# A decoder layer on one core: seven products added up in one PSUM bank, three big PSUM tiles, and changes of order and mode

## The chip, the core and the metric

One core of a Trainium2 chip runs the whole program. The metric is the device time of one execution in microseconds (us), the median of several runs. TensorE (PE) does the matrix products, VectorE (DVE) and ScalarE (ACT) read its results in PSUM, GpSimd (POOL) and SyncE (SP) issue most of the transfers from HBM. PSUM has eight banks of 512 float32 columns on 128 partitions.

## What is computed

One decoder layer on 256 tokens of width 2048 in float32, with all weights read once (about 450 MB):

```python
h = rmsnorm(x, norm_mix)
proj = h @ w_in                        # 30 column blocks of 512, the last 12 are the gates
ya, yb, yr = diff_attention(...), conformer_conv(...), retention(...)
merged = sum(sigmoid(gate_i) * (y_i @ w_branch[i]))
x = x + merged @ w_out
x = x + cross_attention(rmsnorm(x), rmsnorm(mem))   # w_q, w_kv, w_o; 4 heads of 512
a, b = split(rmsnorm(x) @ w13); x = x + (silu(a) * b) @ w2     # hidden 5632
return rmsnorm(x, norm_final)
```

## The kernel before, in words

A weight matrix is cut into blocks of 512 columns (`nb`), each into chunks of 512 rows (`c`), each chunk into halves of 2 x 128 rows. A float32 product is made as three: a value is split into a high part in the engine's reduced format and the rest, and TensorE adds high x high, high x low and low x high in PSUM. So every half of a chunk that arrives as a tile `raw` (512 KB) is cast by ScalarE to `wh` (`hi_of`) and its rest is made by VectorE as `wl` (`lo_of`); five buffers of each (`hlp`) and ten of `raw` (`rawp`) stand between the transfers and TensorE. The activations are the other operand, split in the same way (`Act.hi`, `.lo`).

The program is a list of *units*: a unit is the weights of one half-chunk and its products. `run_items` goes through them; before a unit's products the weights of up to four more units are prepared (`LA = 4`), and after each unit `pump` advances every background *task* (a Python generator: transposes, attention, convolution, normalisation) by one step. A task that holds small PSUM tiles (`TP`, pool `pst`) says so with the number that it yields; `cap` limits their sum, and `drain` runs a task to its end when its result is needed. From this emission order, and the priorities that it gives, a planner lays down the order on each engine before the run; only instructions marked `keep_in_program_order` (the transfers of `ld` on SP and of `gd` on POOL) hold the written order on their engine.

A plain unit ("N") multiplies a half-chunk with both halves of the tokens: 12 products of 512 columns. `block` runs one column block of plain units into a big PSUM tile `mm` (two banks, pool `psm`); `pair_n` runs two column blocks side by side. `pair` runs two column blocks with some chunks ("S", two of four in `MODES2 = "SSNN"`) as a *quad*: seven units of 6 products on sums and differences of the four half-chunks in place of the 48 plain products. The weights' sums come from two additions on VectorE (`f2`, `f3`) and two accumulating transfers on POOL's queue (`gd(..., accum_op=ALU.add)` in `f2` and `f6`); those of the activations are made once by `factors`. Products 2, 3 and 4 of a quad go to the big tiles `ps0` and `ps1`; products 1, 5, 6, 7 go to small tiles of their own (`pp`), and `join1` to `join7` add them together on VectorE into SBUF tiles, to which `done` adds the big tile. There are 26 such pairs: 5 for the gates, 4 for the cross-attention's keys and values, 2 for `w_out`, 1 for `w_o`, 10 in `w_13` and 4 in `w_2`.

PSUM is divided into two big tiles (4 banks) and four small ones (4 banks). `rstd_of` makes an inverse root with one VectorE instruction and a power on GpSimd.

Of the kernel before, what the change touches and what calls it, by code (L numbers as in the profile page):

```python
# [16 lines left out]
D = 2048  # L17
# [40 lines left out]
def trunk(ctx, tc, xT, xtok, memT, memtok, w_in, w_br, w_out, w_q, w_kv, w_o, w_13, w_2,  # L58
# [64 lines left out]
    cap = [4]  # L123
# [169 lines left out]
    def products(u, only=None, final=True):  # L293
        a = u["act"]
        for k in range(2):
            for ps, key, k0, t, kind in u["prods"]:
                if only is not None and t not in only:
                    continue
                ah, al = lhs(a, kind, (t, k0) if kind == "n" else t, k)
                o = ps[key]  # L300
                fl = (id(ps), key)
                pe.matmul(o, ah, u["hi"][:, k, :], start=fl in u["start"] and k == 0, stop=False)
                pe.matmul(o, ah, u["lo"][:, k, :], start=False, stop=False)
                pe.matmul(o, al, u["hi"][:, k, :], start=False, stop=fl in u["stop"] and k == 1)
# [27 lines left out]
    def quad_jobs(pp, ps0, ps1, w0, w1, a):  # L332
# [3 lines left out]
        def unit(ps, key, k0, t, kind, fn, **w):  # L336
            def add():
                load(**w)
                u = add_unit([(ps, key, k0, t, kind)], a)
                u["alloc"] = alloc_tp1 if ps is pp else alloc_mm  # L340
# [3 lines left out]

        def alloc_tp1(ps, key):
            ps[key] = TP()
# [58 lines left out]
    def pair(W0, W1, acts, modes, evac0, evac1):  # L405


        ps0, ps1, pp = {}, {}, {}
# [5 lines left out]
        def enter():  # L414
            settle(3)
            cap[0] = 3
            pin[0] = True

        def join1():
            x0, x1 = S4([P, 2, 512]), S4([P, 2, 512])  # L420
            xs.extend([x0, x1])
            sc.copy(x0[:, 0, :], pp.pop(1))

        def join5():
            ve.tensor_tensor(out=xs[1][:, 1, :], in0=pp.pop(5), in1=xs[0][:, 0, :], op=ALU.add)

        def join6():

            p = pp.pop(6)
            ve.tensor_tensor(out=xs[1][:, 0, :], in0=p, in1=xs[1][:, 1, :], op=ALU.subtract)  # L430
            ve.tensor_tensor(out=xs[0][:, 1, :], in0=p, in1=xs[0][:, 0, :], op=ALU.subtract)

        def join7():
            p = pp.pop(7)
            ve.tensor_tensor(out=xs[0][:, 1, :], in0=p, in1=xs[0][:, 1, :], op=ALU.subtract)
            ve.tensor_tensor(out=xs[1][:, 1, :], in0=xs[1][:, 0, :], in1=p, op=ALU.subtract)
            cap[0] = 4

        def done(n, ps, evac):
            def f():  # L440
                x = xs[n]
                ve.tensor_tensor(out=x, in0=ps["m"], in1=x, op=ALU.add)
                xs[n] = None
                insb[0] = True
                evac(x)
                insb[0] = False
            return f

        call(enter)
        quads = [quad_jobs(pp, ps0, ps1, W0[c], W1[c], acts[c]) for c in sset]  # L450
        n0, n1 = (each_half(ps, [W[c] for c in nset], [acts[c] for c in nset]) for ps, W in ((ps0, W0), (ps1, W1)))

        def units_of(*names):
            return [q[n] for m in names for q in quads for n in m]

        first = units_of(("p1",), ("p2", "p5"), ("p3", "p6"))
        marks = {len(quads) - 1: join1, 3 * len(quads) - 1: join5, 5 * len(quads) - 1: join6}

        def marked(i, f):
            def g():  # L460
                u = f()
                if i in marks:
                    call(marks[i])
                return u
            return g

        us += mixed([marked(i, f) for i, f in enumerate(first)], n0)
        us += [f() for f in units_of(("p7",))]
        call(join7)
        us += mixed(units_of(("p4",)), n1[:len(n1) // 2])  # L470
        call(done(0, ps0, evac0))
        us += [f() for f in n1[len(n1) // 2:]]
        call(done(1, ps1, evac1))

        def unpin():
            pin[0] = False

        call(unpin)
# [36 lines left out]
    def rstd_of(dst, src, scale, w):  # L515
# [3 lines left out]
        nc.gpsimd.tensor_tensor(out=dst, in0=v, in1=nhalf[:, :w], op=ALU.pow)  # L519
# [74 lines left out]
    def factors(a, q):  # L594
# [4 lines left out]
        for o, x, y, op in ((0, a22, a21, ALU.subtract), (2, a11, a21, ALU.subtract),  # L599
                            (1, a22, fv[:, 2], ALU.add), (3, a12, fv[:, 1], ALU.subtract)):  # L600
# [95 lines left out]
    def tok_stats(src, dst, eng):  # L696
# [10 lines left out]
        rstd_of(dst, ss, 1.0 / D, 2)  # L707
# [130 lines left out]
    def conv_norm():  # L838
# [10 lines left out]
        rstd_of(rs, mv.rearrange("p (t s) -> p t s", t=2)[:, :, 1], 1.0, 2)  # L849
# [23 lines left out]
    def win(n0, n1, modes, evac0, evac1):  # L873
# [3 lines left out]
        else:  # L877
# [699 lines left out]
```

## Time and profile before

| what | value |
|---|---|
| time, median of 3 runs | 2031.65 us (2030.2 to 2033.77) |
| the profiled execution | 2031.24 us, its span 2029.5 us |
| TensorE busy | 1990.1 us, 9069 products and transposes |
| VectorE busy | 1680.8 us |
| ScalarE busy | 1122.2 us |
| GpSimd busy | 133.1 us |
| granted TensorE clock, mean | 0.991 |
| read from HBM | 451.73 MB |

Busy time is the union of an engine's instructions. Products overlap in the pipeline (each shows some 0.39 us and the next starts before its end), so a busy TensorE is not one at its peak; an idle figure in square brackets stands before the instruction that ended the wait, with what released it. All compute instructions carry the line of a helper (L86, L94), so groups are told apart by the tiles' names: `wh`, `wl` and `raw` are weights, `mm` and `tp` the big and the small PSUM tiles, `s` SBUF work tiles, `cst_t` the identity for transposes.

### The profile page before, as it was taken

What the parts mean: (1) busy time and instruction counts of PE and PEld (TensorE: products, weight loads), DVE (VectorE), ACT (ScalarE), POOL (GpSimd) and SP (SyncE); (2) the same over time, 40 slices, a digit from 0 to 9 for tenths busy, and PEclk for the clock granted to TensorE, in tenths of its full rate; (3) what the DMA queues carried; (4) which work ended last, traced back from release to release, by engine and by line L of the source; (5) the groups of instructions that cost most, each with busy time, mean ns of one, the idle gap of its engine ahead of it and who ended that gap; (6) DMA issues with size and microseconds to landing.
All of it is one profiled execution on the core that took longest, in us unless ns stands there. A gap on an engine that the chain in (4) does not pass through costs nothing.

```text
span 2029.5 us, 25287 instructions
## 1 busy us (share of the span) xinstructions
PE 1990.1 (98%) x9069; PEld 1641.5 (81%) x9069; DVE 1680.8 (83%) x2049; ACT 1122.2 (55%) x1344; POOL 133.1 (7%) x176
## 2 busy tenths in 40 slices
PE   9999999999999999999999999998999999999998
PEld 7788888888788887778888888886888888878886
DVE  6996689777887787988988565898988899889974
ACT  6434343547465556555656554665655566555653
POOL 0000000000100001011010000100011101011000
PEclk9999999999999999999999999998999999999999
DMA  9555555554677788689999643967899888998891
GB/s 370 189 194 188 176 181 165 181 168 149 176 220 239 243 257 248 226 240 280 284 279 307 208 159 125 288 184 212 226 283 297 257 260 237 289 295 258 262 318 67
DMA packets 128861, 465.97 MB, mean 230 GB/s; under 512 B 14432, under 2 KB 14688, under 8 KB 128736
## 3 DMA queue, kind: packets, MB, share of 16 engines
q1 hardware_dynamic: 105552, 380.46, 53.2%
q0 software_dynamic: 23040, 83.90, 19.5%
q8 instruction: 71, 1.16, 0.2%
q14 instruction: 54, 0.44, 0.1%
q10 hardware_dynamic: 144, 0.01, 0.0%
HBM read 451.73 MB, written 12.58 MB: 229 GB/s over the span
## 4 chain that ended last, share of the span: by engine, by line
PE 50%; issue 9%; DVE 6%; DMA 5%; POOL 1%; ACT 1%; ACTq 0%; POOLq 0%; DVEq 0%
PE mm L86 38%; PE tp L86 12%; DMA raw<-in_w 4%; DVE wl L86 3%; DVE s L86 3%; DMA raw<-in_w_out 1%; DVE raw L86 1%; ACT wh L86 1%; POOL raw L94 1%; DMA s<-in_memtok 0%; DMA raw<-in_w_in 0%; ACT s L86 0%; ACTq L1572 0%; POOL s L94 0%; POOL x2d L94 0%
## 5 line engine op out<-in xcount | busy, mean ns | idle before, releaser
L86 PE MATMUL mm<-wh,s 128*128 128x512 f32 x4528 | 1440.1, 393 | 22.5 <-ACT wh L86 8.7
L86 ACT CAST wh<-raw 128x1024 fp32r<-128x1024 f32 (+1 forms) x861 | 893.6, 1051 | 754.3 <-PE mm L86 462.7
L86 DVE TENSOR_TENSOR wl<-raw,wh 128x1024 fp32r<-128x1024 f32 (+1 forms) x861 | 1030.1, 1220 | 265.2 <-ACT wh L86 252.0
L86 PEld LDWEIGHTS mm<-wh,s 128*128 128x128 f32 x4528 | 854.5, 189 | 204.8 <-ACT wh L86 13.5
L86 PE MATMUL mm<-wl,s 128*128 128x512 f32 x2264 | 889.5, 393 | 7.6 <-DVE wl L86 7.4
L86 PEld LDWEIGHTS mm<-wl,s 128*128 128x128 f32 x2264 | 428.0, 189 | 100.7 <-DVE wl L86 13.2
L86 PE MATMUL tp<-wh,s 128*128 128x512 f32 x896 | 298.5, 392 | 0.0
L86 PEld LDWEIGHTS tp<-wh,s 128*128 128x128 f32 x896 | 168.2, 188 | 34.7 <-issue 0.3
L86 PE MATMUL tp<-wl,s 128*128 128x512 f32 x448 | 174.5, 389 | 0.0
L86 DVE TENSOR_TENSOR s<-s,s 128x1024 f32<-128x1024 f32 (+4 forms) x144 | 141.4, 990 | 5.8 <-ACT s L86 4.0
L86 DVE TENSOR_TENSOR raw<-raw,raw 128x1024 f32<-128x1024 f32 x104 | 126.0, 1220 | 0.5
L86 DVE TENSOR_TENSOR s<-tp,s 128x512 f32<-128x512 f32 (+1 forms) x166 | 110.0, 685 | 19.0 <-PE tp L86 14.2
L86 DVE SCALAR_TENSOR_TENSOR s<-s,prm_t,s 128x256 fp32r<-128x256 f32 (+24 forms) x256 | 105.5, 469 | 0.0
L86 DVE TENSOR_TENSOR s<-mm,s 128x1024 f32<-128x1024 f32 (+1 forms) x71 | 84.4, 1190 | 21.7 <-PE mm L86 21.3
L86 PEld LDWEIGHTS tp<-wl,s 128*128 128x128 f32 x448 | 84.2, 188 | 16.8
L86 ACT ACTIVATE s<-s 128x512 f32<-128x512 f32 (+1 forms) x60 | 46.2, 771 | 64.3 <-DVE s L86 53.9
L94 POOL DMA_DIRECT2D raw<-in_w x56 | 49.4, 882 | 439.4 <-DVE wl L86 187.9
L86 PE MATMUL tp<-cst_t,s 128*128 128x128 f32 x408 | 57.2, 273 | 0.0
L86 PEld LDWEIGHTS tp<-cst_t,s 128*128 128x128 f32 x408 | 48.7, 141 | 9.2 <-issue 0.5
L86 PE MATMUL tp<-s,s 128*128 128x256 f32 (+4 forms) x348 | 54.1, 314 | 0.0
L86 PEld LDWEIGHTS tp<-s,s 128*128 128x128 f32 (+1 forms) x348 | 46.4, 189 | 5.9 <-issue 0.7
L86 ACT COPY s<-tp 128x512 f32<-128x512 f32 (+1 forms) x69 | 35.8, 529 | 21.5 <-PE tp L86 20.0
(88 smaller groups left out, 499.3 us busy)
## 6 DMA issues: line engine op xcount, KB each, us to landing
raw<-in_w SPq DMA_DIRECT2D x264, 512.0 KB, 6.7
raw<-in_w_in SPq DMA_DIRECT2D x239, 512.0 KB, 4.5
raw<-in_w_kv SPq DMA_DIRECT2D x64, 512.0 KB, 6.3
raw<-in_w POOLq DMA_DIRECT2D x56, 512.0 KB, 8.5
raw<-in_w_br SPq DMA_DIRECT2D x48, 512.0 KB, 5.9
raw<-in_w_out SPq DMA_DIRECT2D x32, 512.0 KB, 7.8
raw<-in_w_q SPq DMA_DIRECT2D x32, 512.0 KB, 4.9
raw<-in_w_o SPq DMA_DIRECT2D x32, 512.0 KB, 4.0
```

The lines of the kernel that those rows point to most:

```text
L86: i = f(*a, **k)
L94: tc.keep_in_program_order(nc.gpsimd.dma_start(**kw))
```

## The change

- PSUM becomes three big tiles (6 banks) and two small ones (2 banks); `cap` is 2 throughout.
- In `pair`, products 1, 6, 7 and 4 of the quads go one after the other to the same bank, bank 1 of `ps1`, and product 5 to bank 1 of `ps0`. Between them the bank is copied by ScalarE (`keep1`, `keep5`, `keep6`, `keep7`); `done0` and `done1` combine the copies with the final sums. The two column blocks and the signs in `factors` are exchanged to fit. The units of a pair get a new order: products 1, 2, 5, 3 and the first 6 of both quads come without plain units between them.
- The second pair of start blocks (columns 9 and 7) runs as `pair_n` on the input that is not yet normalised, with the scale applied when the result is read; the normalised input `xn` is made during it.
- One chunk of the first key-value pair and one of the second `w_13` pair become plain (`MODES1 = "SNNN"`).
- `rstd_of` becomes a generator: two rounds pass between VectorE's step and the power, and the power keeps its place in the program order.
- In the last stage three column blocks sum up in big tiles and one in two small tiles, which are claimed once the last hidden chunk is ready.

```diff
-    psm = ctx.enter_context(tc.tile_pool(name="psm", bufs=2, space=bass.MemoryType.PSUM))
+    psm = ctx.enter_context(tc.tile_pool(name="psm", bufs=3, space=bass.MemoryType.PSUM))
-    pst = ctx.enter_context(tc.tile_pool(name="pst", bufs=4, space=bass.MemoryType.PSUM))
+    pst = ctx.enter_context(tc.tile_pool(name="pst", bufs=2, space=bass.MemoryType.PSUM))
-    cap = [4]
+    cap = [2]
...
-                pe.matmul(o, al, u["hi"][:, k, :], start=False, stop=fl in u["stop"] and k == 1)
+                pe.matmul(o, al, u["hi"][:, k, :], start=False, stop=(fl in u["stop"] or "ends" in u) and k == 1, **sk)
...
-        return dict(p1=unit(pp, 1, 0, 0, "n", f1, b11=w0[:, 0:2, :]),
-                    p2=unit(ps0, 0, 2, 0, "n", f2, b21=b21, b12=w1[:, 0:2, :]), p5=unit(pp, 5, 0, 0, "s", f5),
-                    p3=unit(ps1, 0, 0, 3, "s", f3, b22=b22), p6=unit(pp, 6, 0, 1, "s", f6),
-                    p7=unit(pp, 7, 0, 2, "s", f7), p4=unit(ps0, 1, 2, 1, "n", f4))
+        return dict(p1=unit(c1, 1, 0, 0, "n", f1, b11=w0[:, 0:2, :]),
+                    p2=unit(c1, 0, 2, 0, "n", f2, b21=b21, b12=w1[:, 0:2, :]), p5=unit(c2, 1, 0, 0, "s", f5),
+                    p3=unit(c2, 0, 0, 3, "s", f3, b22=b22), p6=unit(c1, 1, 0, 1, "s", f6),
+                    p7=unit(c1, 1, 0, 2, "s", f7), p4=unit(c1, 1, 2, 1, "n", f4))
...
+        def keep1():
+            xs.extend([S4([P, 2, 512]), S4([P, 2, 512])])
+            sc.copy(xs[1][:, 0, :], ps1[1])
+        def keep5():
+            sc.copy(xs[0][:, 0, :], ps0[1])
+        def keep6():
+            sc.copy(xs[1][:, 1, :], ps1[1])
+            ve.tensor_tensor(out=xs[0][:, 0, :], in0=xs[0][:, 0, :], in1=xs[1][:, 1, :], op=ALU.subtract)
+        def keep7():
+            sc.copy(xs[0][:, 1, :], ps1[1])
+        def done0():
+            x = xs[0]
+            ve.tensor_tensor(out=x[:, 0, :], in0=ps0[0], in1=x[:, 0, :], op=ALU.add)
+            ve.tensor_tensor(out=x[:, 1, :], in0=ps0[1], in1=x[:, 1, :], op=ALU.subtract)
...
+        def done1():
+            x = xs[1]
+            ve.tensor_tensor(out=x[:, 0, :], in0=ps1[0], in1=x[:, 0, :], op=ALU.add)
+            sc.copy(x[:, 1, :], ps1[1])
...
+        quads = [quad_jobs(ps1, ps0, W1[c], W0[c], acts[c]) for c in sset]
...
+        us += [f() for f in ending("p1")]
+        call(keep1)
+        us += [f() for f in units_of("p2") + ending("p5")]
+        call(keep5)
+        us += [f() for f in units_of("p3")]
+        p6 = ending("p6")
+        us += mixed(p6[:-1], n0[:-3]) if len(p6) > 1 else [f() for f in n0[:-3]]
+        us.append(p6[-1]())
+        call(keep6)
+        us.append(n0[-3]())
+        us += [f() for f in ending("p7")]
+        call(keep7)
+        us += [f() for f in n0[-2:]]
+        call(done0)
+        us += mixed(units_of("p4"), n1[:len(n1) // 2])
         us += [f() for f in n1[len(n1) // 2:]]
+        call(done1)
...
         ve.tensor_scalar(out=v, in0=src, scalar1=scale, scalar2=EPS, op0=ALU.mult, op1=ALU.add)
-        nc.gpsimd.tensor_tensor(out=dst, in0=v, in1=nhalf[:, :w], op=ALU.pow)
+        yield
+        yield
+        tc.keep_in_program_order(nc.gpsimd.tensor_tensor(out=dst, in0=v, in1=nhalf[:, :w], op=ALU.pow))
...
-        for o, x, y, op in ((0, a22, a21, ALU.subtract), (2, a11, a21, ALU.subtract),
-                            (1, a22, fv[:, 2], ALU.add), (3, a12, fv[:, 1], ALU.subtract)):
+        for o, x, y, op in ((0, a21, a22, ALU.subtract), (2, a11, a21, ALU.subtract),
+                            (1, fv[:, 0], a11, ALU.subtract), (3, a12, fv[:, 1], ALU.add)):
...
-    pair_n([w_in[8, c] for c in range(4)], [w_in[6, c] for c in range(4)], xa, ev_cb(0, rsx), ev_ca(0, rsx),
-           normalise(xa, xn, Rstd(rsx, lambda: drain(st_task)), (), 1))
-    win(9, 7, MODES0, ev_cb(1), ev_ca(1))
+    for n, after in ((0, lambda c: None),
+                     (1, normalise(xa, xn, Rstd(rsx, lambda: drain(st_task)), ()))):
+        pair_n([w_in[8 + n, c] for c in range(4)], [w_in[6 + n, c] for c in range(4)], xa,
+               ev_cb(n, rsx), ev_ca(n, rsx), after)
...
-            pair(w0, w1, mm, MODES2, ev_kv(dst[h]), ev_kv(dst[h + 1]))
+            pair(w0, w1, mm, MODES2 if m or h else MODES1, ev_kv(dst[h]), ev_kv(dst[h + 1]))
...
-                pair(w0, w1, x2n, MODES2, ev_a(i), ev_b(i))
+                pair(w0, w1, x2n, MODES1 if i == 1 else MODES2, ev_a(i), ev_b(i))
...
     def alloc_tp(ps, key):
+        need(hT[10])
+        settle(0)
         ps[0], ps[1] = TP(), TP()
...
-                             alloc=alloc_mm if nb < 2 else alloc_tp))
+                             alloc=alloc_mm if nb < 3 else alloc_tp))
```

For a pair with two quads (a, b) and four plain units for each column block (n, m) the order of the units is, before: 1a 1b 2a n 5a 2b n 5b 3a 6a n 3b 6b n 7a 7b 4a m 4b m m m; after: 1a 1b 2a 2b 5a 5b 3a 3b 6a n 6b n 7a 7b n n 4a m 4b m m m.

## Rows read from the trace of the kernel before

**Rows 1.** The page, busy time of each engine: us, share, count.
```profile
PE 1990.1 (98%) x9069; PEld 1641.5 (81%) x9069; DVE 1680.8 (83%) x2049; ACT 1122.2 (55%) x1344; POOL 133.1 (7%) x176
```

**Rows 2.** Chain in order of time, two steady pairs: start us, us, what.
```profile
1453.99 2.72 PE tp L86 x12
...
1495.72 2.72 PE tp L86 x12
```

**Rows 3.** Windows: stretch, length, each engine's busy us, granted clock, DMA share, GB/s.
```profile
50.00:64.00 14.00, 9.34 (x30) 7.16 (x29) 12.15 (x12) 7.57 (x8) 0.00 (x0) 0.76 0.63 229
543.00:562.00 19.00, 14.27 (x53) 10.81 (x52) 11.98 (x20) 7.45 (x9) 2.51 (x2) 0.82 0.55 148
842.00:874.00 32.00, 26.32 (x103) 19.91 (x102) 28.81 (x34) 14.94 (x18) 2.59 (x3) 0.84 0.65 165
1386.00:1420.00 34.00, 25.22 (x98) 19.97 (x97) 27.16 (x29) 15.18 (x15) 1.70 (x2) 0.85 0.71 219
1453.99:1495.72 41.73, 41.73 (x190) 34.61 (x189) 37.71 (x36) 25.51 (x26) 4.60 (x6) 1.00 0.85 254
```

**Rows 4.** Timeline of TensorE: start us, us, instruction, count, [idle before <-releaser].
```profile
51.78 0.62 PE L86 MATMUL mm<-wh,s 128*128 128x512 f32 x2
...
52.46 0.39 PE L86 MATMUL mm<-wh,s 128*128 128x512 f32 x1
57.51 0.79 PE L86 MATMUL mm<-wh,s 128*128 128x512 f32 x1 [4.66 <-ACT s L86]
...
58.53 1.05 PE L86 MATMUL mm<-wh,s 128*128 128x512 f32 x2
```

**Rows 5.** Timeline of ScalarE at the same place.
```profile
56.19 1.26 ACT L86 ACTIVATE s<-mm,rsx 128x512 f32<-128x512 f32 x2
```

**Rows 6.** Timeline of GpSimd, 528 to 547 us.
```profile
528.88 0.86 POOL L94 DMA_DIRECT2D raw<-in_w_in  x1 [14.54 <-DVE wl L86]
545.35 1.66 POOL L519 TENSOR_TENSOR tn<-tn,nhalf 128x8 f32<-128x8 f32 x1 [15.61 <-DVE tn L86]
546.97 0.89 POOL L94 DMA_DIRECT2D raw<-in_w_in  x1
```

**Rows 7.** Timelines of ScalarE and TensorE, 554 and 555 us.
```profile
554.15 4.83 ACT L86 CAST wh<-raw 128x1024 fp32r<-128x1024 f32 x5 [12.89 <-DMA raw<-in_w_in]
...
555.25 0.80 PE L86 MATMUL mm<-wh,s 128*128 128x512 f32 x1 [3.59 <-ACT wh L86]
```

**Rows 8.** Timeline of TensorE, first key-value pair.
```profile
866.01 0.80 PE L86 MATMUL mm<-wh,s 128*128 128x512 f32 x1 [2.08 <-ACT s L86]
```

**Rows 9.** Groups by shape in one steady pair, VectorE and ScalarE: count, busy us, mean ns.
```profile
L86 DVE TENSOR_TENSOR wl<-raw,wh 128x1024 fp32r<-128x1024 f32 x22 | 26.1, 1220 | 2.9 <-ACT wh L86 2.8
L86 DVE TENSOR_TENSOR raw<-raw,raw 128x1024 f32<-128x1024 f32 x4 | 4.8, 1219 | 0.0
L86 DVE TENSOR_TENSOR s<-tp,s 128x512 f32<-128x512 f32 x4 | 2.7, 686 | 0.8 <-PE tp L86 0.8
L86 DVE TENSOR_TENSOR s<-mm,s 128x1024 f32<-128x1024 f32 x2 | 2.4, 1220 | 0.2 <-PE mm L86 0.2
...
L86 ACT CAST wh<-raw 128x1024 fp32r<-128x1024 f32 x22 | 23.1, 1053 | 15.2 <-PE mm L86 9.7 <-DMA raw<-in_w 2.1 <-PE tp L86 1.4
...
L86 ACT COPY s<-tp 128x512 f32<-128x512 f32 x1 | 0.6, 597 | 0.0
```

**Rows 10.** Timelines of GpSimd, ScalarE, VectorE and TensorE, 1379 to 1412 us.
```profile
1379.25 0.85 POOL L94 DMA_DIRECT2D raw<-in_w  x1 [6.01 <-DMA raw<-in_w]
...
1388.73 3.91 ACT L86 CAST wh<-raw 128x1024 fp32r<-128x1024 f32 x4 [6.14 <-DMA raw<-in_w]
...
1410.51 2.35 DVE L86 TENSOR_TENSOR s<-mm,s 128x1024 f32<-128x1024 f32 x2
...
1411.87 0.76 PE L86 MATMUL mm<-wh,s 128*128 128x512 f32 x1 [7.02 <-DVE s L86]
```

**Rows 11.** The page, issues of accumulating transfers: count, KB each, us to landing.
```profile
raw<-in_w POOLq DMA_DIRECT2D x56, 512.0 KB, 8.5
```

More of the change, by code (lines that the diff above doesn't have):

```diff
@@ L301, in products @@
                 fl = (id(ps), key)
-                pe.matmul(o, ah, u["hi"][:, k, :], start=fl in u["start"] and k == 0, stop=False)
-                pe.matmul(o, ah, u["lo"][:, k, :], start=False, stop=False)
-                pe.matmul(o, al, u["hi"][:, k, :], start=False, stop=fl in u["stop"] and k == 1)
+                sk = dict(skip_group_check=True) if ps.get("open") and key == 1 else {}
+                pe.matmul(o, ah, u["hi"][:, k, :], start=fl in u["start"] and k == 0, stop=False, **sk)
+                pe.matmul(o, ah, u["lo"][:, k, :], start=False, stop=False, **sk)
+                pe.matmul(o, al, u["hi"][:, k, :], start=False, stop=(fl in u["stop"] or "ends" in u) and k == 1, **sk)
     def emit_unit(i):
@@ L343, in unit @@
             return add
-        def alloc_tp1(ps, key):
-            ps[key] = TP()
         b21, b22 = w0[:, 2:4, :], w1[:, 2:4, :]
@@ L396, in f4 @@
             parts(u, t.pop("a"))
[L398 to L401 removed]
+        return dict(p1=unit(c1, 1, 0, 0, "n", f1, b11=w0[:, 0:2, :]),
+                    p2=unit(c1, 0, 2, 0, "n", f2, b21=b21, b12=w1[:, 0:2, :]), p5=unit(c2, 1, 0, 0, "s", f5),
+                    p3=unit(c2, 0, 0, 3, "s", f3, b22=b22), p6=unit(c1, 1, 0, 1, "s", f6),
+                    p7=unit(c1, 1, 0, 2, "s", f7), p4=unit(c1, 1, 2, 1, "n", f4))
     insb = [False]
     def pair(W0, W1, acts, modes, evac0, evac1):
[L408 removed]
+        ps0, ps1 = {"open": True}, {"open": True}
         xs = []
@@ L412, in pair @@
         nset = [c for c in range(len(acts)) if modes[c] == "N"]
[L414 to L447, printed above, removed]
@@ L449, in pair @@
-        call(enter)
-        quads = [quad_jobs(pp, ps0, ps1, W0[c], W1[c], acts[c]) for c in sset]
+        def keep1():
[8 more added lines that the diff above has]
+            sc.copy(xs[0][:, 1, :], ps1[1])
@@ new lines, in done0 @@
+        def done0():
+            x = xs[0]
+            ve.tensor_tensor(out=x[:, 0, :], in0=ps0[0], in1=x[:, 0, :], op=ALU.add)
+            ve.tensor_tensor(out=x[:, 1, :], in0=ps0[1], in1=x[:, 1, :], op=ALU.subtract)
+            xs[0] = None
+            insb[0] = True
+            evac0(x)
+            insb[0] = False
+        def done1():
+            x = xs[1]
+            ve.tensor_tensor(out=x[:, 0, :], in0=ps1[0], in1=x[:, 0, :], op=ALU.add)
+            sc.copy(x[:, 1, :], ps1[1])
+            xs[1] = None
+            insb[0] = True
+            evac1(x)
+            insb[0] = False
@@ L451, in pair @@
+        call(lambda: pin.__setitem__(0, True))
+        quads = [quad_jobs(ps1, ps0, W1[c], W0[c], acts[c]) for c in sset]
         n0, n1 = (each_half(ps, [W[c] for c in nset], [acts[c] for c in nset]) for ps, W in ((ps0, W0), (ps1, W1)))
         def units_of(*names):
[L454 to L463, printed above, removed]
-                return u
-            return g
@@ L467, in pair, with ending, last @@
[L467 to L471, printed above, removed]
+            return [q[n] for n in names for q in quads]
+        def ending(name):
+            fs = units_of(name)
+            def last():
+                u = fs[-1]()
+                u["ends"] = True
+                return u
+            return [f for f in fs[:-1]] + [last]
@@ L472, in pair @@
+        us += mixed(units_of("p4"), n1[:len(n1) // 2])
         us += [f() for f in n1[len(n1) // 2:]]
[L473 to L478, printed above, removed]
+        call(done1)
+        call(lambda: pin.__setitem__(0, False))
         close(us)
@@ L706, in tok_stats @@
         ve.tensor_reduce(out=ss, in_=parts.rearrange("p n t -> p t n"), op=ALU.add, axis=AX.X)
-        rstd_of(dst, ss, 1.0 / D, 2)
+        yield from rstd_of(dst, ss, 1.0 / D, 2)
     def start_task():
@@ L848, in conv_norm @@
         rs = TN(2)
-        rstd_of(rs, mv.rearrange("p (t s) -> p t s", t=2)[:, :, 1], 1.0, 2)
+        yield from rstd_of(rs, mv.rearrange("p (t s) -> p t s", t=2)[:, :, 1], 1.0, 2)
         yield
@@ L969, in ret_task @@
         rs = TN(8)
-        rstd_of(rs, mv.rearrange("p (t s) -> p t s", s=2)[:, :, 1], 1.0, 8)
+        yield from rstd_of(rs, mv.rearrange("p (t s) -> p t s", s=2)[:, :, 1], 1.0, 8)
         yield
@@ L1065, in diff_task @@
         rs = TN(8)
-        rstd_of(rs, ms, 1.0 / P, 8)
+        yield from rstd_of(rs, ms, 1.0 / P, 8)
         yield
@@ L1208, in gen2 @@
                         ve.tensor_reduce(out=ss, in_=parts.rearrange("p n t -> p t n"), op=ALU.add, axis=AX.X)
-                        rstd_of(rs, ss, 1.0 / D, 2)
+                        yield from rstd_of(rs, ss, 1.0 / D, 2)
                     rst[gname] = spawn(gen2())
```

4 lines of the change are left out of this document (2 added, 2 removed).

## The prediction

> **What bounds the kernel now.** I read the page's busy times first. TensorE is busy 1990.1 of 2029.5 us [rows 1], so about 39 us of plain idleness is all that any other engine can give back, plus what idleness does to TensorE's clock. The chain in order of time then gives the price of TensorE's work: twelve products of 512 columns take 2.72 us, 0.227 us each, and the same point of two neighbouring pairs lies 41.73 us apart [rows 2]. A pair is 2 x 42 + 2 x 48 = 180 products, 40.8 us, and some transposes: such a pair holds no wait, as its window says (busy 41.73 of 41.73, clock 1.00, VectorE 37.71) [rows 3]. So nothing can be won in the steady pairs, however much lighter VectorE gets. The windows of the other four stretches show where the time is lost: TensorE idle and then at a granted clock of 0.76 to 0.85 [rows 3]. After the gap at 52 us two products take 1.05 us where they take 0.62 elsewhere [rows 4]: the clock fell from 2.4 to 1.2 GHz in the gap, so a gap costs more than its own length. I price each window as its length less its count times 0.227 us (a little low where transposes are among the count): 14.0 - 30 x 0.227 = 7.2; 19.0 - 53 x 0.227 = 7.0; 32.0 - 103 x 0.227 = 8.6; 34.0 - 98 x 0.227 = 11.8. Together 34.6 us. The question is what ends the wait in each, and whether the change removes that.
>
> **The change, part by part.**
>
> *Third big PSUM tile.* At 52 us the paired start block is over and the next block has no big tile: TensorE resumes at 57.51 us [rows 4], just after ScalarE's sigmoid, which began at 56.19 us, has read the first tile (1.26 us for two pieces) [rows 5]. With a third tile the next products start without it; the second paired block asks for a second tile only two units (5.4 us) later, when the sigmoid is done. Saved: 7.2 of 7.2. The work that moves there is the normalised input: it is now made during the second paired block, one block pair (16 units of 2.72 us, 43.5 us) later, and is needed after it. What it issues (a small broadcast through a PSUM tile, four times three VectorE passes and a ScalarE cast, no DMA) runs beside convolution work; its last two chunks are needed 10.9 and 16.3 us into the next block. I cost it at nothing under that cover; without it, up to the same 7.2 us comes back.
>
> *The power on GpSimd.* At 528.88 us an accumulating transfer is issued, the next only at 546.97, because in between GpSimd's queue stands 15.61 us in a power whose argument VectorE has not made [rows 6]. ScalarE waits 12.89 us for that transfer and TensorE resumes at 555.25 us [rows 7]. The change issues the power two units after VectorE's step and fixes its place in the queue, so the accumulating transfers behind it no longer wait for it. The result comes up to 5.4 us later to tasks that have tens of us. Saved: 7.0 of 7.0.
>
> *First key-value pair.* Around 842 to 874 us VectorE is busy 28.81 of 32 us [rows 3] and TensorE waits for parts and at last, 2.08 us, for a ScalarE cast of the factors [rows 8]. Two things relieve VectorE. The quad that becomes plain loses seven subtractions and two additions and gains four: five passes of 1.19 us (22 take 26.1 us, with their overlap) [rows 9], 5.9 us. The joins fall by 3.1 us, counted below. But the factors of the first chunk are now wanted at the third unit, 2.7 us in, where before it was the fifth, 6.8 us in, and the chain that makes them (statistics, a power, four loads) is not shortened. I take 5.0 of 8.6.
>
> *Second FFN pair.* An accumulating transfer issued at 1379.25 us keeps ScalarE waiting 6.14 us; VectorE falls behind; the closing additions that free the big tiles run at 1410.51 us and TensorE, out of tiles, resumes at 1411.87 us [rows 10]. One quad fewer (5.9 us of VectorE and two accumulating transfers), a third tile, and a longer way from the accumulating transfer to its use all act here. That way, for the second quad's last product, was 9.5 us of TensorE time and becomes 15.0 (counted in the unit orders); such a transfer lands 8.5 us after issue [rows 11]. For the other accumulating transfer it goes from 16.3 to 15.0. Saved: 10.0 of 11.8.
>
> *Two quads made plain* cost six products each: 12 x 0.227 = 2.7 us, certain.
>
> *Joins.* VectorE had per pair five passes over 512 columns (four of 2.7 us together and one of the other form) and two over 1024 of 2.4 [rows 9], 5.8 us; it keeps four of 512, 2.7. ScalarE gets four more copies of about 0.6 us [rows 9], 2.4 us. Both hide in steady pairs, where ScalarE's row has room (25.5 of 41.7 us) [rows 3]. Worth nothing there; if VectorE were the last to finish, it would be 26 x 3.1 = 81 us, and no window of a steady pair shows that.
>
> *The bank read between its products.* Bank 1 of one tile takes product 1, is copied, takes 6, is copied, takes 7, is copied, takes 4. TensorE must wait for each copy. Between product 6 and product 7 lies one plain unit, 2.72 us; after the last 6 comes the latency of a product (0.39 us [rows 4]), perhaps one cast already running on ScalarE (1.05) and the copy (0.60) [rows 9]: 2.0 us, so 0.7 to spare. Two casts in front would leave 0.4 us of wait a pair. The other copies have 4 us and more. I take 0; the bounds are 0 and 0.4 us x 26 = 10 us. The Trainium skill (Perfetto Trace Analysis, section Matmuls) says that independent groups of products should rotate through different PSUM banks, so that the reading of one overlaps the products of the next. That rule speaks against this edit; by it each of the four copies would stand open and the sum would end at the 2073 us of rival 2. The kernel before reads no bank between its products, so its trace doesn't show who is right.
>
> *Order of the units.* A pair now opens with nine short units in a row, 9 x 6 x 0.227 = 12.2 us of TensorE. VectorE needs nine subtractions and four additions for them, 13 x 1.19 = 15.5 us, and still has the last pair's closing (one pass of 512 and one of 1024, 1.9 us). It is 5.2 us short, and lives on a lead: five buffers for the parts let it prepare four units, two additions among them, during the long plain units before (6 x 1.19 = 7.1 us). With a lead of three subtractions alone (3.6 us) 1.6 us a pair would be missing: bounds 0 and 42 us over 26 pairs. Before, plain units stood among the short ones and no wait shows. I take 4 us in all, near the lower end, because the full lead is larger than the shortage and a task's passes eat some of it.
>
> *Two small PSUM tiles instead of four.* Convolution, retention, differential attention and cross-attention share them. Counting the steps in the code, one round per unit, every task still ends before it is needed; the tightest is the second differential attention, which ends three units before the next pair, and the convolution, held up nine times, 25 units ahead of need. The price is TensorE standing in order behind a tile that is read late. There are some 150 such tiles by the code; if every fifth were read one cast (1.05 us) late, that is 30 us, the upper bound; the lower is 0. I take 2: a wait on them appears nowhere now.
>
> The last stage (one more block in a big tile, two small tiles claimed after the last hidden chunk) and the sign changes in the factors issue as many instructions as before: nothing.
>
> Sum, on the profiled execution's own 2031.24 us: - 7.2 - 7.0 - 5.0 - 10.0 + 2.7 + 4 + 2 = -20.5, 2010.7. That execution lies 0.4 us under the median, so I say 2011.
>
> **Rivals.**
> 1. *VectorE falls behind in the run of short units* (the other side). Place: the fifth to ninth unit of each pair. For it: 15.5 against 12.2 us, and pairs whose tasks add factors. Against it: the lead, and 3.1 us less in the pair. From (20.5 + 4) / 26 = 0.9 us a pair the gain is gone; at 1.6 us the time is 2011 - 4 + 42 = 2049. Its place is 2031 to 2049. Chance 0.14.
> 2. *The bank's copy stands open.* At 0.4 us a pair 2021; if all four copies of 0.6 us did, 26 x 2.4 = 62 us, 2073. The rule above would put it towards the far end. Chance 0.10, half under 2027.
> 3. *Tasks starve for small tiles*: 10 to 30 us, 2019 to 2039; for it, the attention stages use more than two at once today; against it, the step count. Chance 0.11, half of it under 2027.
> 4. *The four waits only shrink*, since their causes (late transfers, an order fixed before the run) stay: half of 29 us comes back, 2025. Chance 0.12.
>
> **How the numbers follow.** My forecast, all four waits mostly gone and 6 us of new ones, has 0.53; its own range is 1999 to 2022 (no new waits and 34.6 recovered: 1999.3; twice my new waits and a third less recovered: 2026, taken in part). The range 1996 to 2036 leaves out the far ends of rivals 1 to 3 above and a larger VectorE gain below. Faster by over 0.2% (about what can be told from no change; 4 us): 0.53 + 0.12 + 0.05 + 0.06 = 0.76. Within it 0.08, slower 0.16, from the rest.
>
> **What would show it.** Right: no gap over 1 us near 52 and 551 us; no power between accumulating transfers with a long wait; TensorE's idle under 25 us; pairs 41.7 us apart, and 43.1 for the two with one quad. Wrong: pairs further apart with TensorE waiting for VectorE's parts (rival 1), for ScalarE's copy just before product 7 (rival 2), or small-tile work with waits in front (rival 3).

## The result, and the profile after

The changed kernel takes 2104.46 us (2103.77 to 2106.16, four runs) against 2030.93 us of the kernel before, run beside it: ratio 1.0364, 95% interval 1.0346 to 1.0382. It is 73.5 us slower where 20.5 less were forecast, and outside the range. The page of its profiled execution (span 2104.0 us, mean granted clock 0.982 against 0.991) begins:

```profile
PE 2023.8 (96%) x9081; PEld 1654.3 (79%) x9081; DVE 1618.3 (77%) x1962; ACT 1182.2 (56%) x1447; POOL 132.3 (6%) x172
```

Beside [rows 1], TensorE has the 12 products more that the two plain chunks bring, VectorE is 62.5 us lighter, ScalarE 60 heavier. TensorE's idle share doubled: 80.2 us of the span are without a product where there were 39.4. Windows (columns as in [rows 3]) of the start, of the gate pair at 509 us, of a steady pair and of a long one in `w_13`:

```profile
46.00:60.00 14.00, 14.00 (x66) 11.58 (x65) 8.80 (x10) 7.79 (x9) 0.00 (x0) 1.00 0.83 288
508.70:581.05 72.35, 57.13 (x248) 43.72 (x247) 47.68 (x84) 43.97 (x70) 8.11 (x6) 0.88 0.59 164
1629.30:1670.82 41.52, 41.07 (x181) 33.67 (x180) 34.22 (x31) 26.57 (x28) 4.02 (x5) 1.00 0.85 266
1670.82:1722.15 51.33, 45.94 (x189) 36.35 (x188) 39.38 (x39) 28.35 (x31) 3.45 (x4) 0.93 0.72 204
```

The start wait of [rows 4] is gone (busy 14.00 of 14.00). A steady pair now holds a wait of 0.45 us, and some pairs are 8 to 20 us too long at a clock of 0.88 to 0.93. To see where, I cut both traces at the same counts of 512-column products (every stage has a known number) and set the stages beside each other, in us. The columns behind "after" are experiments, told below. `w_13` pairs are counted from 1.

| stage (its start after) | before | after | side edits | sbuf copy | factors late | own5 | late5 | own5 late5 | all4 |
|---|---|---|---|---|---|---|---|---|---|
| two start blocks (0) | 104.6 | 98.6 | 98.1 | 97.9 | 97.4 | 97.6 | 97.9 | 97.5 | 97.8 |
| gate pair (509) | 52.8 | 72.3 | 44.5 | 59.4 | 73.0 | 63.8 | 71.6 | 63.7 | 44.2 |
| gate pair (668) | 40.8 | 41.6 | 40.8 | 41.0 | 41.6 | 41.6 | 40.8 | 40.8 | 40.8 |
| gate pair (795) | 44.1 | 53.2 | 44.0 | 42.9 | 52.4 | 47.1 | 56.8 | 45.3 | 45.5 |
| first key-value pair (870) | 53.5 | 51.7 | 46.1 | 55.2 | 51.2 | 52.6 | 48.7 | 54.0 | 52.1 |
| w_o pair (1299) | 42.3 | 51.7 | 42.3 | 46.3 | 51.3 | 47.9 | 47.2 | 46.5 | 44.4 |
| w_13 pair 2 (1396) | 43.8 | 54.7 | 43.1 | 43.3 | 54.5 | 45.4 | 54.0 | 45.2 | 46.4 |
| w_13 pair 3 (1450) | 51.9 | 50.4 | 41.7 | 42.6 | 42.6 | 42.6 | 51.4 | 42.6 | 42.7 |
| w_13 pair 4 (1501) | 41.7 | 42.6 | 41.7 | 42.6 | 42.6 | 42.7 | 42.7 | 42.6 | 42.7 |
| w_13 pair 6 (1671) | 41.7 | 51.4 | 42.7 | 42.6 | 42.6 | 42.6 | 48.3 | 42.7 | 42.9 |
| w_13 pair 7 (1722) | 41.7 | 51.3 | 41.8 | 42.7 | 42.7 | 42.7 | 49.9 | 42.6 | 42.6 |

Two more rows move by 7 us and cancel (the four w_q blocks -6.7, the plain part of w_o +7.4). Seven long pairs (one of them, w_13 pair 3, was long already, for the reason in [rows 10]), 0.8 or 0.9 us in most other pairs, less the gains: that is the result.

What happens in a long pair: TensorE in w_13 pair 6 (columns as in [rows 4]), then ScalarE and VectorE at the same place.

```profile
1676.84 0.50 PE L86 MATMUL mm<-wl,s 128*128 128x512 f32 x1 [0.67 <-DVE wl L86]
...
1682.58 0.50 PE L86 MATMUL mm<-wl,s 128*128 128x512 f32 x1 [1.36 <-DVE wl L86]
...
1685.98 0.50 PE L86 MATMUL mm<-wl,s 128*128 128x512 f32 x1 [1.75 <-DVE wl L86]
...
1689.03 0.79 PE L86 MATMUL mm<-wh,s 128*128 128x512 f32 x1 [1.62 <-ACT s L86]
...
1690.40 1.05 PE L86 MATMUL mm<-wh,s 128*128 128x512 f32 x2
```
```profile
1677.01 0.60 ACT L86 COPY s<-mm 128x512 f32<-128x512 f32 x1
...
1687.45 1.04 ACT L86 CAST wh<-raw 128x1024 fp32r<-128x1024 f32 x1 [2.37 <-PE mm L86]
1688.40 0.58 ACT L86 COPY s<-mm 128x512 f32<-128x512 f32 x1
1688.88 1.05 ACT L86 CAST s<-s 128x1024 fp32r<-128x1024 f32 x1
1689.82 0.59 ACT L86 COPY s<-mm 128x512 f32<-128x512 f32 x1
```
```profile
1675.57 3.49 DVE L86 TENSOR_TENSOR wl<-raw,wh 128x1024 fp32r<-128x1024 f32 x3
...
1683.57 1.22 DVE L86 TENSOR_TENSOR s<-s,s 128x1024 f32<-128x1024 f32 x1
1684.71 1.22 DVE L86 TENSOR_TENSOR wl<-raw,wh 128x1024 fp32r<-128x1024 f32 x1
1685.85 0.75 DVE L86 TENSOR_TENSOR s<-s 128x256 f32<-128x256 f32 x2
```

The three copies `s<-mm` are `keep1`, `keep6` and, last, `keep5`: by the program's order on ScalarE, product 5's copy stands behind product 6's and straight behind the cast `s<-s` of a task's factors, 12.8 us after `keep1`. Until this copy has run, from 1689.82 on, nothing more is written to the first big tile: product 3, whose parts VectorE had made by 1679.1, and the plain units run after it. So TensorE has only the two units of product 6, whose parts VectorE makes just then between the factors' passes, and waits for each (1.36, 1.75); product 7 needs the same bank and waits for `keep6` (1.62). After that two products take 1.05 us, the clock is at 1.2 GHz. In a steady pair `keep5` comes 5.4 us after `keep1`; there TensorE waits for it as well, and the next product to run is one of product 3:

```profile
1638.26 0.50 PE L86 MATMUL mm<-wh,s 128*128 128x512 f32 x1 [0.45 <-ACT s L86]
```
```profile
1637.62 0.59 ACT L86 COPY s<-mm 128x512 f32<-128x512 f32 x1
```

Nine pairs show this wait (0.61 us from the time that the product was due; such a pair takes 41.56 us in place of 40.80). In the pair at 509 us the longest wait is another one: a small-tile transpose of the differential attention stands in TensorE's order ahead of the pair's products, and its input is late on VectorE:

```profile
523.88 0.48 PE L86 MATMUL tp<-cst_t,sm 128*128 128x128 f32 x1 [8.41 <-DVE sm L86]
```

The attention itself is late: the power of its closing normalisation, at 545.35 us before [rows 6], comes after this pair has ended.

```profile
584.45 1.66 POOL L524 TENSOR_TENSOR tn<-tn,nhalf 128x8 f32<-128x8 f32 x1 [49.06 <-DVE tn L86]
```

### The profile page after: what moved, and what is told of

Same layout as the page of the kernel before. It is cut to its first block, busy times and chain, and to the rows that moved or that the text cites. A ratio compares the mean times of both kernels' runs of the same rounds, so it can differ in the third digit from the quotient of the medians.

```text
span 2104.0 us, 25310 instructions
## 1 busy us (share of the span) xinstructions
PE 2023.8 (96%) x9081; PEld 1654.3 (79%) x9081; DVE 1618.3 (77%) x1962; ACT 1182.2 (56%) x1447; POOL 132.3 (6%) x172
## 4 chain that ended last, share of the span: by engine, by line
PE 88%; DVE 6%; ACT 2%; issue 2%; DMA 1%; SPq 0%; ACTq 0%; POOLq 0%; POOL 0%; DVEq 0%
PE mm L86 83%; PE tp L86 5%; DVE wl L86 3%; DVE s L86 2%; ACT wh L86 1%; DVE raw L86 1%; ACT s L86 1%; DMA x2d<-s 1%; DMA raw<-in_w_in 0%; DMA raw<-in_w 0%; DMA raw<-in_w_o 0%; DVE tn L86 0%; SPq L97 0%; ACT sm L86 0%; ACT L86 0%
## 5 line engine op out<-in xcount | busy, mean ns | idle before, releaser
L86 PE MATMUL mm<-wh,s 128*128 128x512 f32 x5400 | 1704.7, 395 | 29.8 <-ACT s L86 26.6
L86 PEld LDWEIGHTS mm<-wh,s 128*128 128x128 f32 x5400 | 1023.2, 190 | 257.4 <-ACT s L86 38.4
L86 PE MATMUL mm<-wl,s 128*128 128x512 f32 x2700 | 1065.5, 395 | 22.0 <-DVE wl L86 21.8
L86 PEld LDWEIGHTS mm<-wl,s 128*128 128x128 f32 x2700 | 512.6, 190 | 136.9 <-DVE wl L86 31.6
L86 DVE SCALAR_TENSOR_TENSOR s<-s,prm_t,s 128x228 f32<-128x228 f32 (+23 forms) x256 | 106.3, 465 | 0.0
L86 DVE TENSOR_TENSOR s<-mm,s 128x512 f32<-128x512 f32 (+1 forms) x98 | 72.6, 763 | 39.9 <-PE mm L86 39.8
L86 ACT COPY s<-mm 128x512 f32<-128x512 f32 x130 | 75.9, 586 | 21.9 <-PE mm L86 16.8
L86 DVE TENSOR_TENSOR s<-tp,s 128x512 fp32r<-128x512 f32 (+1 forms) x60 | 40.1, 684 | 10.5 <-ACT s L86 6.6
L86 ACT CAST s<-tp 128x512 fp32r<-128x512 f32 x58 | 32.2, 586 | 15.9 <-PE tp L86 15.7
L86 ACT CAST s<-s 128x1024 fp32r<-128x1024 f32 (+1 forms) x32 | 29.7, 941 | 8.0 <-DVE s L86 8.0
L86 ACT COPY s<-tp 128x512 f32<-128x512 f32 (+1 forms) x43 | 20.5, 491 | 22.1 <-PE tp L86 21.9
```

What stands on the lines that cost most here:

```text
L86: i = f(*a, **k)
```

## The experiments

Theories: **V**, VectorE is behind in the run of short units, above all where a task adds passes (rival 1). **B**, TensorE waits for the copies of the open bank (rival 2). **S**, two small tiles make the tasks late, and their transposes block TensorE (rival 3). Edits are against the changed kernel but in the first, and are shown shortened. Times without an interval are of a single execution; the kernel before varied from 2027 to 2036 us over all its runs.

**side_only**: the kernel before with `pair_n` twice at the start, `MODES1` in the two pairs, and the late power:

```diff
-    win(9, 7, MODES0, ev_cb(1), ev_ca(1))
+    for n, after in ((0, lambda c: None), (1, normalise(...))):   # pair_n on columns 8, 6 and 9, 7
-            pair(w0, w1, mm, MODES2, ...)        # and in w_13
+            pair(w0, w1, mm, MODES2 if m or h else MODES1, ...)
+        yield
+        yield
+        tc.keep_in_program_order(nc.gpsimd.tensor_tensor(out=dst, in0=v, in1=nhalf[:, :w], op=ALU.pow))
```

> The kernel before (its own pair, two big and four small PSUM tiles) with three edits of the change alone: the second start pair as two paired blocks on the input that is not yet normalised, one plain chunk more in the first key-value pair and in the second w_13 pair, and the power on GpSimd two rounds later and in program order. Nothing is left out of the computation. If these edits carry their part of my sum by themselves (power 7.0 us, perhaps 3 to 5 us in each of the two pairs, less 2.7 us of added products; the start wait stays or moves, since there is no third big tile) the time is 2015 to 2025 us, ratio 0.992 to 0.997. If they only pay together with the new pair and its third tile, it is 2028 to 2035, ratio 0.999 to 1.002. Either way it says how much of the 73 us lost must belong to the pair and the PSUM split.

Measured: 2000.81 us (1997.57 to 2003.0), ratio 0.9851, interval 0.983 to 0.9872. That is faster than either of my bands. The edits alone give 29.5 us, and need neither the new pair nor the third tile: the start has no wait with two big tiles either. So the new pair and the PSUM split cost 2104.5 - 2000.8 = 103.7 us. Windows of its start, of the gate pair and of w_13 pair 3, to set beside [rows 3]:

```profile
48.00:62.00 14.00, 14.00 (x66) 11.58 (x65) 10.18 (x14) 6.19 (x7) 0.00 (x0) 1.00 0.78 271
509.60:554.10 44.50, 43.36 (x199) 35.32 (x198) 40.43 (x54) 31.88 (x42) 4.29 (x3) 1.00 0.74 231
1380.00:1421.70 41.70, 41.70 (x189) 34.61 (x188) 39.74 (x42) 26.32 (x27) 2.59 (x3) 1.00 0.81 248
```

The power that waited 15.61 us among the accumulating transfers [rows 6] waits a third of that:

```profile
532.94 2.57 POOL L521 TENSOR_TENSOR tn<-tn,nhalf 128x8 f32<-128x8 f32 x1 [5.28 <-DVE tn L86]
```

**small4**:

```diff
-psm bufs=3, pst bufs=2, cap = [2]
+psm bufs=2, pst bufs=4, cap = [4]      # and the last stage as before
```

> The changed kernel with the PSUM split of before: two big tiles and four small ones, tasks allowed to hold four, last stage as before. Nothing is left out. Theory S (the two small tiles make the background tasks late, so that their transposes stand in TensorE's order in front of late VectorE work): the losses of the gate pair at 508 to 581 us (+19.5 us) and of the one at 795 to 849 us (+9.1) vanish, the start wait of 7 us comes back: 2080 to 2088 us. Theory V (VectorE falls behind in the run of short units wherever a task adds passes) and theory B (TensorE waits for the copies of the bank): those losses stay, 2100 to 2115 us.

Measured: 2059.38 us. The gate pair at 509 us falls from 72.3 to 45.0 us, the w_o pair by 7.1, the first key-value pair by 5.9. But the gate pair at 795 us keeps 52.5, and w_13 pairs 3, 6 and 7 their 50 to 51 us. S holds for the first only; the time lies below its band, and the w_o and key-value pairs, which it had not named, gain too. The start wait does not return. The power of the late attention is back inside the gate pair (510.2 to 555.2 us):

```profile
536.00 2.57 POOL L524 TENSOR_TENSOR tn<-tn,nhalf 128x8 f32<-128x8 f32 x1 [10.09 <-DVE tn L86]
```

**copy_sbuf**:

```diff
-            sc.copy(xs[0][:, 0, :], ps0[1])            # keep5; keep6 and keep7 likewise
+            sc.copy(xs[0][:, 0, :], xs[1][:, 0, :])
```

> The changed kernel in which the three copies of the open bank after products 5, 6 and 7 read an SBUF tile of the same size in its place; the copy after product 1 stays. It leaves out those three readings, so the sums that use them are not the layer's. ScalarE and VectorE do as many instructions as in the changed kernel. Theory B (TensorE waits for ScalarE's copy before it may write the bank again, some 0.6 us in most pairs and 2 to 3 us in a few): 12 to 25 us less, 2080 to 2092 us, and the rows of TensorE that wait 0.6 us for ScalarE in the steady pairs are gone. Theory V: these waits are slack that the next wait for VectorE takes up again, 2098 to 2106 us.

Measured: 2043.51 us, 61 less, over twice B's upper end. VectorE is busy 1610.9 us, as in the changed kernel within 8, and the w_13 pairs that had waited for its parts stand at 42.6. In w_13 pair 6, which starts at 1627.4 us, product 5's copy and product 7's, which goes into the same tile, come even later than in the changed kernel (20.4 us after `keep1`), again behind the cast of the factors:

```profile
1650.83 1.05 ACT L86 CAST s<-s 128x1024 fp32r<-128x1024 f32 x1
...
1654.02 1.14 ACT L86 COPY s<-s 128x512 f32<-128x512 f32 x2
```

But they read no bank, and TensorE does not wait. So V is not the root: VectorE's lateness costs little as long as TensorE has other units to run.

**factors_late**:

```diff
+                    for _ in range(10):
+                        yield
                     yield from add_factors(hT[i])
```

> The changed kernel in which the task that makes a hidden chunk's factors waits ten rounds more before it starts adding them, so that VectorE does that work after the next pair's run of short units and not in it; the transposes stay where they were. Nothing is left out. Theory V (the factors' VectorE passes in the run of short units are what makes pairs 1, 5 and 6 of w_13 each 9.5 to 11 us longer): those three pairs come to within 2 us of the others, 2075 to 2085 us. Theory B or S: these pairs stay 9 us longer, 2100 to 2110 us.

Measured: 2079.66 us; w_13 pairs 3, 6 and 7 fall to 42.6; pair 2, which V had named too (the expectation counts from 0), stays. That is V's number, yet the run before had cured the same pairs without touching VectorE. Both edits have one thing in common: `keep5` no longer matters, or no longer stands behind the factors' cast. This led to theory **P**: no work tile is free for `keep5`.

**own5** and its control **raw9**:

```diff
-rawp bufs=10
+rawp bufs=9                                            # raw9: this line alone
+k5p = tc.tile_pool(name="k5p", bufs=2)
-            sc.copy(xs[0][:, 0, :], ps0[1])
+            xs.append(k5p.tile([P, 512], F32, ...)); sc.copy(xs[2], ps0[1])
-            ve.tensor_tensor(out=xs[0][:, 0, :], in0=xs[0][:, 0, :], in1=xs[1][:, 1, :], op=ALU.subtract)
+            ve.tensor_tensor(out=xs[0][:, 0, :], in0=xs[2], in1=xs[1][:, 1, :], op=ALU.subtract)
```

> The changed kernel in which the copy of product 5 goes to a small SBUF pool of its own (two tiles of 2 KB) instead of the shared pool of 28 work tiles; to make room, nine weight buffers instead of ten. Nothing is left out of the computation. The trace of the changed kernel shows that copy at the right place in the steady pairs (some 5.4 us after the copy of product 1) but 12 to 13 us after it in the long pairs, behind the copy of product 6 and straight behind the casts of a background task's factors. Theory P (the copy waits for a free work tile, which the task's temporaries hold, and everything that writes the first big tile waits for the copy): the long pairs lose most of their 8 to 10 us, 2050 to 2075 us, and the wait of 0.6 us of the steady pairs stays. Theory V (VectorE is simply behind): the long pairs stay, 2095 to 2110 us.

> The changed kernel with nine weight buffers instead of ten and nothing else changed, beside which the run with product 5's own pool is read. The transfers have one buffer less of lead: 2104 to 2112 us, and the long pairs stay where they are. If it is faster than 2095 us or slower than 2115, the other run can't be read as the effect of the pool alone.

Measured: 2052.94 us, and 2097.3 for the control, which was 7 us faster where I had expected up to 8 slower; its long pairs stay. Beside it, product 5's own pool gives 44 us. ScalarE in w_13 pair 6 now, `k<-mm` being `keep5`, 2.3 us after `keep1`, and the pair's window:

```profile
1643.19 0.60 ACT L87 COPY s<-mm 128x512 f32<-128x512 f32 x1
1644.49 1.06 ACT L87 CAST wh<-raw 128x1024 fp32r<-128x1024 f32 x1 [0.70 <-PE mm L87]
1645.45 0.57 ACT L87 COPY k<-mm 128x512 f32<-128x512 f32 x1
```
```profile
1637.00:1679.70 42.70, 42.03 (x190) 34.68 (x189) 38.67 (x39) 28.17 (x31) 3.45 (x4) 1.00 0.82 246
```

VectorE does 38.67 us of work in it, as in the long pair (39.38), and TensorE is idle 0.67.

**late5**:

```diff
-        us += [f() for f in units_of("p2") + ending("p5")]
-        call(keep5)
-        us += [f() for f in units_of("p3")]
+        us += [f() for f in units_of("p2") + ending("p5") + units_of("p3")]
+        call(keep5)
```

> The changed kernel with the copy of product 5 written after the two units of product 3 instead of before them. Nothing is left out. Product 3 goes to the other bank of the same big tile, so it does not need the copy by the computation. Theory B (it is product 3, the next unit of the same big tile, that waits 0.6 us for the copy in each steady pair): these waits go, 12 to 16 us, and the long pairs have 2.7 us more of work that may run before the copy: 2075 to 2092 us. If the wait belongs to the plain units behind it, or if the next wait takes its place, 2100 to 2106 us.

Measured: 2083.41 us, 21 less: B's number, though the nine pairs with the steady wait give only about 7.6 us of it and the long pairs the rest (w_o 4.5, w_13 pair 6 3.1). The steady gate pairs are at 40.80 us, which is 180 products of 0.227 us and no wait. This window shows it:

```profile
664.95:705.75 40.80, 40.80 (x182) 33.78 (x181) 32.12 (x29) 25.77 (x27) 1.70 (x2) 1.00 0.85 277
```

**own5_late5**: both edits.

> Both edits together: product 5's copy in its own pool, written after product 3, with nine weight buffers. Nothing is left out. If P and B are two separate losses they add up: 2035 to 2060 us, what remains being the attention tasks on two small PSUM tiles (about 27 us in the gate pair at 508 us). If VectorE is the limit behind both, less than two thirds of the two gains together.

Measured: 2041.57 us; from the control 55.7 us of the 65.4 that the two give singly, in the forecast band. The gate pair at 509 us keeps 63.7.

**all4**: own5_late5 with small4's PSUM split.

> The changed kernel with product 5's copy in its own pool and after product 3 (nine weight buffers), and the PSUM split of before: two big tiles, four small ones, tasks allowed to hold four. Nothing is left out. Theory S (what is left of the loss, 19 us in the gate pair at 508 us, 4 in the w_o pair, a few near 600 and 850 us, comes from the two small tiles): 2005 to 2015 us, ratio to the kernel before 0.987 to 0.992. If the third big tile is worth something by itself, the start wait of 6 us returns and it ends near 2015 to 2020. If VectorE in the run of short units is behind these losses, 2030 us or more. Against the kernel with the side edits alone (2000.8 us) it says what the new pair costs or gives when nothing holds its copies up.

Measured: 2018.76 us (2016.59 to 2020.78), ratio 0.9946, interval 0.9927 to 0.9964. The gate pair is at 44.2 us, S's part; but it ends above S's band, and no start wait explains that. What is left against the side edits is seen in the table: 6 us in the first key-value pair and 0.9 in most w_13 and w_2 pairs. TensorE in two of these places:

```profile
838.28 0.77 PE L87 MATMUL mm<-wh,s 128*128 128x512 f32 x1 [3.71 <-ACT s L87]
```
```profile
1398.74 0.50 PE L87 MATMUL mm<-wl,s 128*128 128x512 f32 x1 [0.66 <-DVE wl L87]
```

The first waits for the first cast of the factors. With the side edits alone this cast comes no earlier, the pair begins 1.9 us sooner (830.2 against 832.2 us), and TensorE doesn't wait for it: the old order of the units asks for the factors later. So this wait belongs to the new order. First the cast in all4, then in side_only:

```profile
837.18 1.04 ACT L87 CAST s<-s 128x1024 fp32r<-128x1024 f32 x1
```
```profile
840.57 1.05 ACT L86 CAST s<-s 128x1024 fp32r<-128x1024 f32 x1 [2.50 <-DVE s L86]
```

(In small4 the same order shows only 45.7 us in this pair: the gate pair ahead had taken 7 us more than in all4, and the cast, at 838.2 us, was done before the pair began.) The second waits for VectorE's parts in the run of short units, right behind the last pair's closing pass:

```profile
1395.20 1.22 DVE L87 TENSOR_TENSOR s<-s,s 128x1024 f32<-128x1024 f32 x1
1396.34 1.22 DVE L87 TENSOR_TENSOR raw<-raw,raw 128x1024 f32<-128x1024 f32 x1
1397.47 3.48 DVE L87 TENSOR_TENSOR wl<-raw,wh 128x1024 fp32r<-128x1024 f32 x3
```

P had a rival by now, **Q**: the pool's tiles are handed out in the order in which the kernel writes their first uses, so `keep5`, the first write of its tile, waits its turn behind the first write of a task's tile, free tiles or not.

**work30**:

```diff
-s4 bufs=28, rawp bufs=10
+s4 bufs=30, rawp bufs=8
```

> The changed kernel with 30 work tiles in the shared SBUF pool instead of 28, and eight weight buffers instead of ten to make room. Nothing is left out. Theory P as it was put before (no work tile is free when product 5's copy wants one): the long pairs of the FFN lose their 8 us each as they did with a pool of its own, 2045 to 2065 us. Theory Q (tiles of the pool are handed out in the order in which the kernel writes their first uses, so the copy, the first write of its tile, waits behind the first write of the factors' last tile, whether or not a tile is free): two tiles more change nothing, the copy stays behind the factors' cast, 2085 to 2110 us.

**claim**:

```diff
+            sc.copy(xs[0][:, 0, 0:2], ps1[1][:, 0:2])     # in keep1, ahead of its own copy
             sc.copy(xs[1][:, 0, :], ps1[1])
```

> The changed kernel with one more ScalarE copy per pair, of two columns, into the tile of product 5's copy, written right before the copy of product 1: the tile's first write is then there, and product 5's copy is only its second. No memory is added or taken. The two columns are overwritten later, so nothing is left out of the computation. Theory Q: the long pairs shrink as with the pool of its own, 2045 to 2075 us, though nothing about the number of free tiles has changed. Theory P: unchanged or worse, since the tile is held for longer, 2095 to 2115 us.

Measured: work30 2096.19 us, the copy still straight behind the factors' cast; claim 2069.43. ScalarE in w_13 pair 6 of work30:

```profile
1682.88 0.58 ACT L86 COPY s<-mm 128x512 f32<-128x512 f32 x1
1683.36 1.05 ACT L86 CAST s<-s 128x1024 fp32r<-128x1024 f32 x1
1684.30 0.59 ACT L86 COPY s<-mm 128x512 f32<-128x512 f32 x1
```

P falls, Q stands: two tiles more change nothing, two columns written early give 35 us. (The early write alone would not tell P from Q, since it also takes the tile early; work30 does.) The Trainium skill (Perfetto Trace Analysis, section Identifying Performance Opportunities) says that the same gap repeating on the engine that should be saturated can mean too little SBUF or PSUM for the next tile. Here, as far as these runs tell, the bubbles did come from the hand-out of tiles, but not from their number.

**claim_all**: claim, late5 and small4's PSUM split together.

> That early first write together with product 5's copy after product 3 and the PSUM split of before (two big, four small tiles), ten weight buffers. Nothing is left out. It should end where the same combination with a pool of its own did, 2010 to 2022 us, ratio to the kernel before 0.991 to 0.997; against the side edits alone (2000.8 us) the new pair then still costs 10 to 20 us, from VectorE 0.7 us behind after the transposes in each of ten FFN pairs and from the factors of the first key-value pair that are wanted earlier.

Measured: 2027.6 us (2024.33 to 2029.61), ratio 0.9986, interval 0.9976 to 0.9995, 6 us above the band. Against all4 the two w_2 pairs whose tiles hang on a store take 44.4 and 44.2 us for 41.2. In claim the same place shows ScalarE itself held up, by a store that must leave the tile:

```profile
1567.15 0.58 ACT L86 COPY s<-mm 128x512 f32<-128x512 f32 x1 [4.68 <-DMA x2d<-s]
```

So an early first write is not free: it also asks for the tile early. The fastest of all kernels here is the one with the side edits alone.

## Why the prediction was wrong, step by step

**The four waits: right in sum, partly by luck.** The side edits alone measure the terms: 26.5 us forecast, 29.5 measured. Start: 104.6 to 98.1, 6.5 us for my 7.2. Power: the gate pair and the stage ahead of it fall from 129.4 to 122.8, 6.6 for 7.0. First key-value pair: 53.5 to 46.1, a net 7.4 with its six added products, where 5.0 less 1.4 was forecast. Second FFN pair, whose gap falls into the next when cut by products: 95.7 to 84.8 over the two, a net 10.9 for 10.0 less 1.4. So the last two gave 3.8 and 2.3 us more than forecast, and not for all my reasons: I had counted on lighter joins in the one, on a third tile and a longer way for the accumulating transfers in the other, and the side edits have none of these. The start needs no third tile either.

**The step that failed is "The bank read between its products".** I looked at products 6 and 7, found 0.7 us to spare, and wrote "The other copies have 4 us and more. I take 0; the bounds are 0 and 0.4 us x 26 = 10 us". Between 6 and 7 there is indeed no wait in a steady pair. But the "4 us and more" of product 5's copy fits only if it is counted, by the order of the units, up to the plain units, the next users of its bank (two units of product 3 and one of product 6 stand in between, 4.1 us). The program makes product 3 wait, which goes to the other bank of the same tile and comes straight after. That is the 0.61 us of nine pairs, gone in late5, and by itself (5.5 us of waiting) within my bounds. What broke the bound is that I gave the copy a time (product's latency, a cast, the copy) and no place in an order: its tile is handed out behind a task's tiles, and in w_13 pair 6 it came 12.8 us after `keep1`. Undoing this place gives 44 us beside its control (own5), or 35 with no change of memory (claim). With the copy also written after product 3, 55.7 us go (raw9 to own5_late5): that is what the term cost that I took at 0.

**Two small PSUM tiles: the mechanism was rival 3's, my size wrong.** I took 2 us of a range to 30; it costs 45 us alone (small4), 22.8 of them still with the copies cured (own5_late5 to all4). My count of steps said that the second differential attention ends three units before the next pair; its transposes stand in that pair, waiting 8.41 us for VectorE at the head of TensorE's order, and its closing power comes at 584.45 us, after the pair. Even before, that power stood inside the pair (545.35), so the count was wrong there too.

**The order of the units: a term mis-sized.** 4 us taken. With copies and tiles cured (all4 against side_only) 0.9 us in most w_13 and w_2 pairs and 3.3 in w_13 pair 2, about 7 in all, and 6 us in the first key-value pair, whose factors are wanted at the third unit, as I had written without charging it enough.

**The sum in place of mine**, each step from one run to the next: 2104.5, weight buffers -7.2, product 5's place -44.4, its copy after product 3 -11.4, small tiles -22.8, what the new pair and its pools still cost -18.0, which is the 2000.8 of the side edits. The steps were taken in one order and overlap; what a weight buffer fewer does for 7.2 us I did not pursue, and of the last 18.0 the 6 and the 7 us above are placed. No run has the old order of the units with products added up in one bank, so what the order costs and what the copies on ScalarE cost in these 7 us is not told apart.

**The rivals.** Rival 2 was right that the bank's copy stands open, wrong that it would do so evenly in all pairs. The rule of the Trainium skill (Perfetto Trace Analysis, section Matmuls) to rotate independent groups through banks so that the reading of one overlaps the products of the next points the right way: where the next unit went to the copied tile at once, TensorE waited 0.61 us; where other units stood between (late5), the same four copies cost nothing in a pair of 40.80 us. Rival 1's sign, parts from VectorE in front of TensorE's waits, is in the rows, but the run with copies from SBUF shows that it was a consequence. Rival 4 is out: the side edits alone took the waits away.

What is not shown: how the planner hands out tiles. Q is inferred from three runs that replaced a first write (own5), put one earlier (claim) or moved the task's behind (factors_late), and from one that added tiles in vain (work30).

## What to carry to other kernels

Sharing one accumulator turns every evacuation into a link of TensorE's own chain: list for each copy the next writer of the same tile (not only of the same bank) and what the copy itself must wait for, its destination included. Where an order is planned from emission, a first write into a shared pool may queue behind a background task's first writes, as these runs suggest; try a pool of its own for such a copy. And test the harmless edits of a bundle alone: here they were worth 29.5 us, and the bold part hid it.

## What the runs showed unexpectedly

Reading a bank between products of one chain costs TensorE nothing when at least one unit (1.36 us) to another tile stands behind the last product: 40.80 us for a pair with four such copies, the same as the pair of before with none. And small waits close together cost more than their sum: in w_13 pair 6 waits of 1.36, 1.75 and 1.62 us were followed by some 5 us in which two products took 1.05 us, 1.2 GHz, where 0.62 is the rule.
